# Tanh forms of Gelu and sigmoid tile by tile, state-space units with second buffers, and output low parts on VectorE, in a one-core hybrid layer

## The chip, the cores and the metric

The kernel runs on one core of one Trainium2 chip. The metric is the time of one execution on the device in microseconds, the median of several runs. Engines are named as the profile names them: PE is TensorE (matmuls), PEld its loading of weights, DVE VectorE, ACT ScalarE, POOL GpSimd, SP the engine whose queue starts most DMAs.

## The reference, cut to what matters

One layer of a network of width 1024 over 2048 tokens, in float32. One norm and one input projection feed two mixers, whose outputs are normalised, joined, projected by `w_out` and added to the stream; a SwiGLU feed-forward layer and a last norm follow.

```python
h = rmsnorm(x, norm_mix_g); proj = h @ w_in          # u_ssm 512 | q 512 | k 512 | v 512
# mixer A: 32 groups of 16 channels, one diagonal complex state of 64 per group
_, states = lax.associative_scan(combine, (a, bu), axis=1)
y = einsum(states, c_mat).real + d_skip * uf
y = jax.nn.gelu(y)                                   # the tanh form
y_ssm = y * jax.nn.sigmoid(y @ w_glu + b_glu)
# mixer B: 8 heads of 64, each chunk of 64 tokens sees itself and the 8 chunks before it
y_att = softmax(q k / 8 + bias) v
mixed = concat(rmsnorm(y_ssm, g_ssm), rmsnorm(y_att, g_att))
x = x + mixed @ w_out
h2 = rmsnorm(x, norm_ffn_g)
x = x + (silu(h2 @ w_gate) * (h2 @ w_up)) @ w_down
return rmsnorm(x, norm_final_g)
```

## The kernel before, in words

Nearly every matmul is done in three passes on high and low parts, so that float32 accuracy is kept: `split` makes the high part with a cast on ACT (L165) and the low part as a difference on DVE or POOL (L166), and `mm3` issues high x high, high x low and low x high. All PE matmuls are recorded at L74, transposes and spreads at L77.

The 2048 tokens are four blocks of 512 (`sb`). The program has these stages, with their place in the span in microseconds: the first projections (to about 155), attention with the state-space units and the later projections in between (155 to 743), the mixing (685 to about 950), gate and up (to 1840) and down (to 2303). A tile framework schedules the instructions of each engine by the order of the program and by due times; the matmuls of attention are kept in the order of the program. A pool reuses a tile's space when the last reader of the tile is done, and a transfer into the tile waits for that.

**Attention** (`att_phase`) is a hand-written loop of 128 steps, each one head of a quarter block: scores, masked softmax (`mn` on DVE L846, exponentials on ACT L849), transposes into `pt`, its parts `pth` (ACT L864) and `ptl` (DVE L865), and after four steps the product with v. Between these pieces the loop advances `Unit`s: generators with `n` yields that are spread over the steps `s0` to `s1`, the first piece `pre` steps earlier. Units compute the projections of later blocks, the state-space scan, and, at the end, the first part of the mixing.

**State-space units** (`ssm_unit`, eight of them, b = 0 to 7, four groups each): load U (the inputs), Bst, Tm and Vm; matmuls U x Bst into PSUM `pj`, copied by ACT to X (8 copies, L591); a recursion over 256 chunks of 8 tokens on POOL (L605 to L608 and L616, L617) in 7 + 7 + 3 + 4 pieces; X is moved by POOL's DMA queue into XG; matmuls U x Tm and XG x Vm, copied by ACT to Y (2 copies, L649) and stored to `y`. Before, each of these tiles has one buffer, and Y is a second tile under the tag of X. A unit starts every SW = 15 steps and spans 15. SP issues the loads of a unit when its first piece is run; Tm and Vm are loaded with U.

**Mixing** (`mix_phase`). For each block: `load` fetches y (`yr`) and applies Gelu into `ys`, `split` makes `gh`, `gl`; `load_a` fetches attention's output `ya` and `squares` sums its squares; `glu` multiplies by w_glu (parts `wgh`, `wgl`), adds the bias `bg`, takes the sigmoid and multiplies `ys`; `rstd1` sums squares by matmuls with ones and finds the reciprocal root by Newton steps on DVE (L115 to L123, result `no`); `rstd2` scales by gain; `mixed` makes the parts `m`; `split_wo` makes the parts `woh`, `wol` of w_out once; `w_out` multiplies and adds x. The matmuls of block 0's and 1's GLU write to the banks `pf` and `big`. The tag `sg` is a ring of SGB = 2 temporaries of 128x512, used by w_glu's raw tiles, by the squares and by sigmoid.

In blocks 0 and 1 Gelu is one ACT instruction over 128x2048 (L1034), and the sigmoid is `late`: DVE adds the bias into `yr` (L1061), one ACT instruction over 128x2048 does the sigmoid (L1063), and DVE multiplies (L1065). In blocks 2 and 3 both are done tile by tile (L1034, L1068, L1069). Gelu, sigmoid and the exponential of softmax lie in different tables of ACT, so that a change between them brings an ACT_TABLE_LOAD into ACT's order. The mixing's unit is opened at step OPEN = 119; its loads are issued at once, its pieces from GSTART = 122 on.

Of the kernel before, what the change touches and what calls it, by code (L numbers as in the profile page):

```python
# [12 lines left out]
AF = mybir.ActivationFunctionType  # L13
ALU = mybir.AluOpType
AX = mybir.AxisListType

P = 128
# [3 lines left out]
NG, CH, NS = 32, 16, 64  # L21
NPR = NG // 2
L = 8
NC = SEQ // L
GB, GP = 4, 2
H, HD = 8, 64
SB = 512
# [4 lines left out]
EPS = 1e-6  # L32
LAG = 2
WB = 3
OPEN, GSTART = 119, 122
R1 = 13
SGB = 2
ON_POOL = 2, 5, 7
RA1, RA2 = 2, 12
# [5 lines left out]
SL = 1  # L45
LPH = 2
V0 = 0, 4
DB, XB = 3, 2
SW = 15
CUT = -8, -2, 2, 7, 13, 19, 24  # L50
CUTL = -8, -2, 2, 7, 13, 19, 23
ORDER = "sptf"
# [1 line left out]
YL = 8  # L54
YX = 9
# [51 lines left out]
def f32(ap):  # L107
    return ap.bitcast(F32)
# [54 lines left out]
def split(k, hi, lo, raw, lo_eng=None, hi_eng=None):  # L163
    nc = k.nc
    (hi_eng or nc.scalar).copy(hi, raw)  # L165
    (lo_eng or nc.gpsimd).tensor_tensor(lo, raw, f32(hi), op=ALU.subtract)  # L166
# [393 lines left out]
def ssm_unit(k, p, psum, S, b, eng):  # L560

    nc = k.nc
    F = GB * CH
    U = k.t(p, "U", [P, GB, NC])

    def load(out, in_):
        ins = nc.sync.dma_start(out, in_)
        if b == 0:
            k.tc.keep_in_program_order(ins)
# [7 lines left out]
    for i in range(L):  # L577
        load(tm[i * CH : (i + 1) * CH], S["kt"].rearrange("c g a m -> c g (a m)")[:, gs, P - CH * i : 2 * P - CH * i])
    vm = k.t(p, "Vm", [P, GB, P])
    load(vm[:], S["v"].rearrange("q g c n m -> (c n) (q g) m")[:, gs, CH:])  # L580
# [39 lines left out]
    for s in range(1, 8):  # L620
        step(Xk[:, :, :, :, s], Xk[:, :, :, :, s - 1], 0, NC // 8)
        yield
    for b_ in range(1, 8):
        step(Xe[:, :, :, :, b_], Xe[:, :, :, :, b_ - 1], 1, 4)
        yield
# [13 lines left out]
            eng.dma_start(XGv[c * NS : (c + 1) * NS, :, g2, 1:], X[g2 * NS : (g2 + 1) * NS, c, :, : NC - 1])  # L639
    for _ in range(YX):  # L640
        yield
    Y = k.t(p, "X", [P, GB, NC])
    for q in range(GP):
        ps = k.t(psum, "pj", [P, 2, NC], bufs=2)
        for g2 in range(2):
            g = 2 * q + g2
# [6 lines left out]
        yield  # L653


SSM_N = YL + GP + 7 + 7 + 3 + 4  + YX + GP


class Unit:
# [21 lines left out]
def att_phase(k, ident, S):  # L681
    tc, nc, io = k.tc, k.nc, k.io
    with ExitStack() as cx:
# [245 lines left out]
        sp = tc.alloc_tile_pool(name="ssm", reuse_waits="tile", bufs=1)  # L929
        psum = cx.enter_context(tc.tile_pool(name="aps", bufs=1, space=bass.MemoryType.PSUM, reuse_waits="tile"))  # L930
        psum2 = cx.enter_context(tc.tile_pool(name="aps2", bufs=1, space=bass.MemoryType.PSUM, reuse_waits="tile"))
        units = []
# [9 lines left out]
                      Unit(qk_unit(sb, 2), QK_N, g0 + C[3], g0 + C[4], 2, light=LIGHT), Unit(v_unit(sb, 1), V_N, g0 + C[4], g0 + C[5], 2, light=LIGHT),  # L942
                      Unit(qk_unit(sb, 3), QK_N, g0 + C[5], g0 + C[6], 2, light=LIGHT)]
        for b in range(NG // GB):
            units.append(Unit(ssm_unit(k, sp, psum, S, b, k.ssm_eng), SSM_N, 2 + int(SW * b), 2 + int(SW * (b + 1)), light=SL))
# [24 lines left out]
MIX_N = 17 + PY + PZ  # L970


def mix_phase(k, S, bank):

    tc, nc, io = k.tc, k.nc, k.io
    te = k.te
    with ExitStack() as cx:
# [28 lines left out]
        def squares(src):  # L1006
            sq = k.t(mz, "sq", [P, SB], bufs=2)
            for f in range(4):
                if f == 0:
                    nc.scalar.activation(sq[:], src[f], AF.Square)  # L1010
                else:
                    t = k.t(mz, "sg", [P, SB], bufs=SGB)
                    nc.scalar.activation(t[:], src[f], AF.Square)
                    (nc.gpsimd if f == 2 else nc.vector).tensor_tensor(sq[:], sq[:], t[:], op=ALU.add)
            return sq

# [2 lines left out]

        yrs = [None]  # L1020

        def load(sb, one=False):
# [8 lines left out]
            yv = b.yr = yrs[0][:, :, :, (sb % 2) * 64 : (sb % 2 + 1) * 64]  # L1031
            fs = [slice(0, 4)] if one else [slice(f, f + 1) for f in range(4)]
            for s in fs:
                nc.scalar.activation(yt[:, s].rearrange("p f (c j) -> p f c j", j=L), yv[:, s].rearrange("p f j c -> p f c j"), AF.Gelu_apprx_tanh)  # L1034
# [12 lines left out]
        def glu(b, bank, late=False):  # L1047


            def by8(a):  # L1050
                return a.rearrange("p (a b) -> p a b", a=L)

            for f in range(4):
                ps = bank()
                cs = slice(f * P, (f + 1) * P)
                for q in range(4):
                    mm3(te, ps[:, :512], Wg[q][0][:, cs], Wg[q][1][:, cs], b.g[q][0][:], b.g[q][1][:], q == 0, q == 3)
                    if q < 3:
                        yield
                if late:  # L1060
                    nc.vector.tensor_scalar(b.yr[:, f], by8(ps[:, :512]), bg[:, f : f + 1], None, op0=ALU.add)  # L1061
                    if f == 3:
                        nc.scalar.activation(b.yr, b.yr, AF.Sigmoid)  # L1063
                        for i in range(4):
                            nc.vector.tensor_tensor(by8(b.ys[i]), by8(b.ys[i]), b.yr[:, i], op=ALU.mult)  # L1065
                else:
                    sg = k.t(mz, "sg", [P, SB], bufs=SGB)
                    nc.scalar.activation(sg[:], ps[:, :512], AF.Sigmoid, bias=bg[:, f : f + 1])  # L1068
                    nc.vector.tensor_tensor(b.ys[f], b.ys[f], sg[:], op=ALU.mult)  # L1069
                yield  # L1070
            b.sqs = squares(b.ys)

        def rstd1(b, c, ps):

# [73 lines left out]
        b = load(0, True)  # L1148
# [4 lines left out]
        for n, _ in enumerate(glu(b, bank, True)):  # L1153
# [7 lines left out]
        nxt = load(1, True)  # L1161
        for _ in range(PZ):
            yield

# [2 lines left out]
            psum = k.psum  # L1167
            return bank() if psum is None else big()

        for n, _ in enumerate(glu(nxt, bk, True)):  # L1170
            if n == R1:
                rstd1(b, 1, bk())
            yield
# [531 lines left out]
```

## Time and profile before

| | before |
|---|---|
| time, median of 3 runs | 2308.74 us (2308.12 to 2310.45) |
| the profiled execution's own time | 2304.9 us |
| its span | 2303.1 us |
| mean granted clock of TensorE | 0.975 |
| busy PE / PEld / DVE / ACT / POOL | 2183.8 / 1834.1 / 1487.8 / 1001.3 / 1061.0 us |
| bytes moved by DMA | 437 MB, mean 190 GB/s |

The profile is of one execution. In its lists, a line has the line of the program, engine, operation, output and inputs, shape, and how many; a timeline has start and length in microseconds, and in brackets how long the engine was idle before, and what ended it. A table of waits has engine, waiting line, what it waited for, and then the total in microseconds, the number and the longest. The granted clock is a share of full speed.

### The profile page before, as it was taken

The numbers are of one execution on the slowest core, as the hardware profiler recorded it, in microseconds if no ns is written. First come the engines' busy times: TensorE is split into PE (matmuls) and PEld (weight loads), VectorE is DVE, ScalarE is ACT, GpSimd is POOL, SyncE is SP. The second block draws the span as 40 slices with busy tenths as digits, with TensorE's granted clock in tenths as the row PEclk, the third lists the DMA queues.
The fourth block names the chain that finished last, engine by engine and source line by source line (L and its number), as shares of the span: only waits on it lengthen the run. The fifth ranks groups of instructions, "written<-read, shape, count | busy, mean of one in ns | idle before, by whom it ended". The sixth has DMA issues, their size and how long they took to land.

```text
span 2303.1 us, 30454 instructions
## 1 busy us (share of the span) xinstructions
PE 2183.8 (95%) x10568; PEld 1834.1 (80%) x10568; DVE 1487.8 (65%) x2286; ACT 1001.3 (43%) x1675; POOL 1061.0 (46%) x1245
## 2 busy tenths in 40 slices
PE   8978799999997899989999999999999999999997
PEld 6667688898986788778888887888888878888886
DVE  7845555656555756676775669766645376578676
ACT  6335555555557542343333335333333343344332
POOL 3416655455660433265555554555555314445442
PEclk9989999999998999999999999999999999999998
DMA  8788766766653534754554556555433287465552
GB/s 295 260 286 265 235 210 204 207 190 193 192 137 114 178 118 163 249 165 143 167 193 157 205 190 254 195 193 167 158 96 110 76 326 265 165 228 183 201 182 74
DMA packets 216370, 437.00 MB, mean 190 GB/s; under 512 B 27352, under 2 KB 58120, under 8 KB 209112
## 3 DMA queue, kind: packets, MB, share of 16 engines
q1 hardware_dynamic: 211352, 420.89, 55.0%
q0 software_dynamic: 4864, 14.17, 1.9%
q8 instruction: 83, 1.36, 0.2%
q14 instruction: 71, 0.58, 0.1%
HBM read 294.98 MB, written 132.15 MB: 185 GB/s over the span
## 4 chain that ended last, share of the span: by engine, by line
PE 59%; DVE 3%; DMA 1%; ACT 1%; issue 1%; POOL 1%; SPq 0%; DVEq 0%; ACTq 0%; POOLq 0%
PE X L74 20%; PE ps L74 18%; PE Y L74 10%; PE big L74 6%; PE W L74 5%; DVE acc L1575 1%; DMA lo<-hc 0%; DMA x<-xt 0%; DVE xt L1117 0%; DVE lo L166 0%; DVE hd L166 0%; POOL c L166 0%; ACT hi L165 0%; POOL sa L1125 0%; DMA gl<-x 0%
## 5 line engine op out<-in xcount | busy, mean ns | idle before, releaser
L74 PE MATMUL X<-hi,c 128*128 128x512 f32 x1408 | 452.2, 392 | 7.6 <-ACT u L1391 3.5
L74 PE MATMUL ps<-hd,hd 128*128 128x512 f32 (+1 forms) x1968 | 431.7, 381 | 3.9 <-DVE hd L166 3.7
L74 PEld LDWEIGHTS ps<-hd,hd 128*128 128x128 f32 x1968 | 358.8, 190 | 75.5 <-DVE hd L166 5.1
L166 POOL TENSOR_TENSOR c<-S,c 128x512 fp32r<-128x512 f32 x176 | 253.1, 1440 | 260.7 <-ACT c L165 258.8
L74 PEld LDWEIGHTS X<-hi,c 128*128 128x128 f32 x1408 | 265.8, 189 | 65.2 <-ACT u L1391 5.1
L74 PE MATMUL X<-lo,c 128*128 128x512 f32 x704 | 275.3, 391 | 0.0
L166 POOL TENSOR_TENSOR hd<-hd 128x1536 fp32r<-128x1536 f32 (+1 forms) x46 | 159.1, 3463 | 232.0 <-ACT hd L165 218.8
L166 POOL TENSOR_TENSOR c<-raw,c 128x512 fp32r<-128x512 f32 x132 | 189.0, 1432 | 137.5 <-ACT c L165 109.1
L165 ACT CAST hd<-hd 128x1536 fp32r<-128x1536 f32 (+1 forms) x106 | 147.4, 1393 | 219.4 <-DMA hd<-hq 134.5
L74 PE MATMUL Y<-hi,c 128*128 128x512 f32 x704 | 225.5, 391 | 4.8 <-DVE u L1395 4.8
L1521 DVE TENSOR_TENSOR acc<-acc,ps 128x512 f32<-128x512 f32 x196 | 129.2, 681 | 79.5 <-PE ps L74 79.1
L74 PE MATMUL big<-m,woh 128*128 128x512 f32 x512 | 165.4, 404 | 0.6 <-DVE m L166 0.4
L165 ACT CAST c<-S 128x512 fp32r<-128x512 f32 x176 | 109.5, 622 | 116.5 <-PE Y L74 59.1
L74 PE MATMUL pf<-hi,w 128*128 128x512 f32 x416 | 150.9, 415 | 9.4 <-ACT hi L729 5.8
L74 PEld LDWEIGHTS Y<-hi,c 128*128 128x128 f32 x704 | 132.6, 188 | 33.9 <-DVE u L1395 6.3
L74 PEld LDWEIGHTS X<-lo,c 128*128 128x128 f32 x704 | 133.0, 189 | 27.7
L1391 ACT COPY u<-X 128x512 f32<-128x512 f32 x132 | 77.1, 585 | 177.5 <-PE X L74 177.5
L846 DVE CUSTOM_DVE_ANT_0 s<-sc,nb 128x640 f32<-128x640 f32 (+4 forms) x128 | 94.4, 737 | 89.4 <-PE sc L74 85.9
L605 POOL TENSOR_TENSOR st<-X,a 128x128 f32<-128x128 f32 (+2 forms) x136 | 47.4, 349 | 220.0 <-ACT X L591 157.4
L165 ACT CAST c<-raw 128x512 fp32r<-128x512 f32 x132 | 82.1, 622 | 143.1 <-PE Y L74 80.3
L166 DVE TENSOR_TENSOR hd<-hd 128x1536 fp32r<-128x1536 f32 (+1 forms) x60 | 119.3, 1990 | 31.2 <-ACT hd L165 30.5
L74 PE MATMUL Y<-lo,c 128*128 128x512 f32 x352 | 137.2, 390 | 0.0
(462 smaller groups left out, 4644.2 us busy)
## 6 DMA issues: line engine op xcount, KB each, us to landing
w<-wss SPq DMA_DIRECT2D x36, 1024.0 KB, 5.5
hq<-g SPq DMA_DIRECT2D x140, 256.0 KB, 2.1
hd<-hq SPq DMA_DIRECT2D x42, 768.0 KB, 4.5
hd<-wc SPq DMA_DIRECT2D x42, 768.0 KB, 6.0
raw<-in_w_gate SPq DMA_DIRECT2D x44, 512.0 KB, 3.7
raw<-in_w_up SPq DMA_DIRECT2D x44, 512.0 KB, 4.1
wc<-px SPq DMA_DIRECT2D x66, 256.0 KB, 3.2
wss<-w SPq DMA_DIRECT2D x12, 1024.0 KB, 5.6
```

What stands on the lines that cost most here:

```text
L74: return self.tc.keep_in_program_order(self.tc.nc.tensor.matmul(*a, **b))
L165: (hi_eng or nc.scalar).copy(hi, raw)
L166: (lo_eng or nc.gpsimd).tensor_tensor(lo, raw, f32(hi), op=ALU.subtract)
L605: eng.tensor_tensor(t[:, :, :, :n], src, ar, op=ALU.mult)
L846: nc.vector.tensor_tensor_reduce(s[:, :nk].rearrange("p (a b) -> p a b", a=nch), ps[:, :nch, :half], hd.nb[:, nk - 1 :: -1].rearrange("p ( ...
L1391: nc.scalar.copy(u[:], ps[:])
L1521: V.tensor_tensor(a, a, ps[:], op=ALU.add)
L1575: nc.vector.scalar_tensor_tensor(v, v, k.go[:, i : i + 1], self.rs[:, : self.n], op0=ALU.mult, op1=ALU.mult)
```

## The change

It has five parts, made at once.

1. The state-space units: U gets two buffers, Y a tile of its own; a unit starts every 14 steps and spans 15, so that neighbours overlap by one step; the first piece of units 1 to 7, the loads of U and Bst, is run four steps early; their Tm and Vm are loaded after the first seven pieces of the recursion; seven empty yields fall away.
2. The mixing's unit starts at step 121 instead of 122 with fewer empty yields, and its window ends one step earlier; the units' pool is released at step 119 instead of 122.
3. Gelu is computed per tile of 128x512 as y(1 + tanh(c(y + 0.044715 y^3))), twice its value: Square and Tanh on ACT, two scalar-tensor-tensor instructions on DVE, of which the second writes with a step of eight elements; the factor 0.5 goes into `gh` and `gl`. The sigmoid becomes 1 + tanh(z/2), twice its value, straight from PSUM for all blocks, with one DVE instruction per tile. The gain `gs` is scaled by 0.25 and the bias by 0.5 for this. The late path is removed. Temporaries come from the ring `sg`.
4. The low parts of w_out (four of eight) and of `m` (16 of 32) that POOL computed move to DVE.
5. The scratch space of POOL's DMA queue is set to 8192 bytes.

ACT's order holds nine ACT_TABLE_LOADs before and two after. Every line number of the changed kernel is one or more higher (L74 becomes L75, L1034's place is taken by L1044 to L1047).

```diff
-OPEN, GSTART = 119, 122
-R1 = 13
+OPEN, GSTART = 119, 121
+R1 = 9
+CUBE = 0.044715
-SW = 15
+SW, SPAN = 14, 15
...
-    U = k.t(p, "U", [P, GB, NC])
+    U = k.t(p, "U", [P, GB, NC], bufs=2)
...
-    tm = k.t(p, "Tm", [P, GB, P])
...
-    for _ in range(YL):
+    if b == 0:
+        tm, vm = load_tv()
+    for _ in range(YL if b == 0 else 1):
         yield
...
         step(Xk[:, :, :, :, s], Xk[:, :, :, :, s - 1], 0, NC // 8)
         yield
+    if b:
+        tm, vm = load_tv()
...
-    Y = k.t(p, "X", [P, GB, NC])
+    Y = k.t(p, "Y", [P, GB, NC])
...
-            units.append(Unit(ssm_unit(...), SSM_N, 2 + int(SW * b), 2 + int(SW * (b + 1)), light=SL))
+            s0 = 2 + SW * b
+            units.append(Unit(ssm_unit(...), SSM_N if b else SSM_N + YL - 1, s0, s0 + SPAN, 4 if b else 0, light=SL))
...
-                units += [Unit(islice(mix, MIX_N), MIX_N, GSTART, N + LAG, GSTART - OPEN)]
-            if s == GSTART:
-                sp.release()
+                sp.release()
+                units += [Unit(islice(mix, MIX_N), MIX_N, GSTART, N + 1, GSTART - OPEN)]
...
-PY, PZ = 8, 1
-MIX_N = 17 + PY + PZ
+PY, PZ = 3, 1
+MIX_N = 16 + PY + PZ
...
+        nc.vector.tensor_scalar(gs[:], gs[:], 0.25, None, op0=ALU.mult)
+        nc.vector.tensor_scalar(bg[:], bg[:], 0.5, None, op0=ALU.mult)
...
-                split(k, W[q][0][:], W[q][1][:], raw[:], nc.vector if n % 2 else nc.gpsimd)
+                split(k, W[q][0][:], W[q][1][:], raw[:], nc.vector)
...
-                nc.scalar.activation(yt[:, s].rearrange(...), yv[:, s].rearrange(...), AF.Gelu_apprx_tanh)
             for f in range(4):
+                t = k.t(mz, "sg", [P, L, SB // L], bufs=SGB)
+                nc.scalar.activation(t[:], yv[:, f], AF.Square)
+                nc.vector.scalar_tensor_tensor(t[:], t[:], 1 / CUBE, yv[:, f], op0=ALU.add, op1=ALU.mult)
+                nc.scalar.activation(t[:], t[:], AF.Tanh, scale=CUBE * math.sqrt(2 / math.pi))
+                nc.vector.scalar_tensor_tensor(b.ys[f].rearrange("p (c j) -> p j c", j=L), t[:], 1.0, yv[:, f], op0=ALU.add, op1=ALU.mult)
-                split(k, gh[:], gl[:], b.ys[f], nc.vector)
+                nc.scalar.activation(gh[:], b.ys[f], AF.Copy, scale=0.5)
+                nc.vector.scalar_tensor_tensor(gl[:], b.ys[f], 0.5, f32(gh[:]), op0=ALU.mult, op1=ALU.subtract)
...
-                if late:
-                    nc.vector.tensor_scalar(b.yr[:, f], by8(ps[:, :512]), bg[:, f : f + 1], None, op0=ALU.add)
-                    if f == 3:
-                        nc.scalar.activation(b.yr, b.yr, AF.Sigmoid)
-                        for i in range(4):
-                            nc.vector.tensor_tensor(by8(b.ys[i]), by8(b.ys[i]), b.yr[:, i], op=ALU.mult)
-                else:
-                    nc.scalar.activation(sg[:], ps[:, :512], AF.Sigmoid, bias=bg[:, f : f + 1])
-                    nc.vector.tensor_tensor(b.ys[f], b.ys[f], sg[:], op=ALU.mult)
+                nc.scalar.activation(sg[:], ps[:, :512], AF.Tanh, bias=bg[:, f : f + 1], scale=0.5)
+                nc.vector.scalar_tensor_tensor(b.ys[f], sg[:], 1.0, b.ys[f], op0=ALU.add, op1=ALU.mult)
-            b.sqs = squares(b.ys)
+            b.sqs = squares(b.ys, 0.25)
...
-                split(k, mh, ml, y, nc.gpsimd if n % 2 else nc.vector)
+                split(k, mh, ml, y, nc.vector)
...
-        load_wg()
-        yield
+        load_wg()
...
-    nc = bacc.Bacc("TRN2", target_bir_lowering=False, num_devices=1)
+    nc = bacc.Bacc("TRN2", target_bir_lowering=False, num_devices=1, dynamic_dma_scratch_size=8192)
```

Two places where the order of the instructions changes. The first is ACT at the boundary of two state-space units (X from L591, Y from L649, whose tile is still called X before; pth and s belong to attention, v and k to later projections). Before:

```order
L649 COPY X_4155<-pj_4156 128x512
L649 COPY X_4155<-pj_4162 128x512
L864 CAST pth_4124<-pt_4185 128x5x128
L849 ACTIVATE s_4181,sm_3828<-s_4181,mn_4182 128x640
...
L804 CAST v_1008_4071<-pf_4247 128x4x64
L591 COPY X_4308<-pj_4309 64x256 x4
L591 COPY X_4308<-pj_4316 64x256 x4
L849 ACTIVATE s_4330,sm_4236<-s_4330,mn_4331 128x640
```

After:

```order
L657 COPY Y_4063<-pj_4064 128x512
L857 ACTIVATE s_4039,sm_3876<-s_4039,mn_4040 128x640
L657 COPY Y_4063<-pj_4070 128x512
L597 COPY X_4084<-pj_4085 64x256 x4
L597 COPY X_4084<-pj_4092 64x256 x4
L872 CAST pth_3981<-pt_4114 128x5x128
```

The copies of the outgoing unit and those of the incoming one stood apart, with attention's exponentials between; now they follow each other, and one pth stands behind all ten.

The second is DVE from the end of block 0's GLU on (ptl of attention, gl of block 1, yr the bias added for block 0). Before:

```order
L865 TENSOR_TENSOR ptl_8526<-pt_8600,pth_8525 128x5x128
L1061 TENSOR_SCALAR yr_8351<-pf_8584,bg_8214 128x8x64
L166 TENSOR_TENSOR gl_1991_8634<-ys_8631,gh_1990_8633 128x512
L166 TENSOR_TENSOR gl_1993_8638<-ys_8631,gh_1992_8637 128x512
L166 TENSOR_TENSOR gl_1995_8642<-ys_8631,gh_1994_8641 128x512
```

After, where sq and sg are squares and temporaries of the ring, and ys_8647 is block 1's output of Gelu:

```order
L1024 TENSOR_TENSOR sq_8636<-sq_8636,sg_8644 128x512
L1045 SCALAR_TENSOR_TENSOR sg_8648<-sg_8648,yr_8273 128x512
L1045 SCALAR_TENSOR_TENSOR sg_8657<-sg_8657,yr_8273 128x512
L1047 SCALAR_TENSOR_TENSOR ys_8647<-sg_8648,yr_8273 128x8x64
L1047 SCALAR_TENSOR_TENSOR ys_8647<-sg_8657,yr_8273 128x8x64
L1050 SCALAR_TENSOR_TENSOR gl_1999_8654<-ys_8647,gh_1998_8653 128x512
```

Before, the four gl of block 1 follow at once on block 0's last bias; now block 1's Gelu, four tiles of two instructions each, stands in front of its gl, behind the squares of block 0.

More of the change, by code (lines that the diff above doesn't have):

```diff
@@ L575, in ssm_unit, with load_tv @@
     load(bst[:].rearrange("p g m -> p (g m)"), S["bst"][b // 2][:, (b % 2) * GB * P : (b % 2 + 1) * GB * P])
-    tm = k.t(p, "Tm", [P, GB, P])
[L577 to L580, printed above, removed]
-    for _ in range(YL):
+    def load_tv():
+        tm = k.t(p, "Tm", [P, GB, P])
+        for i in range(L):
+            load(tm[i * CH : (i + 1) * CH], S["kt"].rearrange("c g a m -> c g (a m)")[:, gs, P - CH * i : 2 * P - CH * i])
+        vm = k.t(p, "Vm", [P, GB, P])
+        load(vm[:], S["v"].rearrange("q g c n m -> (c n) (q g) m")[:, gs, CH:])
+        return tm, vm
+    if b == 0:
+        tm, vm = load_tv()
+    for _ in range(YL if b == 0 else 1):
         yield
@@ L653, in ssm_unit @@
         yield
-SSM_N = YL + GP + 7 + 7 + 3 + 4  + YX + GP
+SSM_N = 1 + GP + 7 + 7 + 3 + 4  + YX + GP
 class Unit:
@@ L944, in att_phase @@
         for b in range(NG // GB):
-            units.append(Unit(ssm_unit(k, sp, psum, S, b, k.ssm_eng), SSM_N, 2 + int(SW * b), 2 + int(SW * (b + 1)), light=SL))
+            s0 = 2 + SW * b
+            units.append(Unit(ssm_unit(k, sp, psum, S, b, k.ssm_eng), SSM_N if b else SSM_N + YL - 1, s0, s0 + SPAN, 4 if b else 0, light=SL))
         N = len(steps)
@@ L1003, in split_wo, with squares @@
                 raw = raws[n] if n < len(raws) else load_wo(n, wr, "xt")
-                split(k, W[q][0][:], W[q][1][:], raw[:], nc.vector if n % 2 else nc.gpsimd)
-        def squares(src):
+                split(k, W[q][0][:], W[q][1][:], raw[:], nc.vector)
+        def squares(src, scale=1.0):
             sq = k.t(mz, "sq", [P, SB], bufs=2)
@@ L1009, in squares @@
                 if f == 0:
-                    nc.scalar.activation(sq[:], src[f], AF.Square)
+                    nc.scalar.activation(sq[:], src[f], AF.Square, scale=scale)
                 else:
                     t = k.t(mz, "sg", [P, SB], bufs=SGB)
-                    nc.scalar.activation(t[:], src[f], AF.Square)
+                    nc.scalar.activation(t[:], src[f], AF.Square, scale=scale)
                     (nc.gpsimd if f == 2 else nc.vector).tensor_tensor(sq[:], sq[:], t[:], op=ALU.add)
@@ L1020, in mix_phase, with load @@
         yrs = [None]
-        def load(sb, one=False):
+        def load(sb):
             b = B()
@@ L1030, in load @@
                     nc.sync.dma_start(yrs[0][:, f], S["y"][f * P : (f + 1) * P, :, sb * 64 : sb * 64 + 128])
[L1031 to L1034, printed above, removed]
+            yv = yrs[0][:, :, :, (sb % 2) * 64 : (sb % 2 + 1) * 64]
             for f in range(4):
+                t = k.t(mz, "sg", [P, L, SB // L], bufs=SGB)
[3 more added lines that the diff above has]
+                nc.vector.scalar_tensor_tensor(b.ys[f].rearrange("p (c j) -> p j c", j=L), t[:], 1.0, yv[:, f], op0=ALU.add, op1=ALU.mult)
                 gh, gl = k.t(my, f"gh{f}", [P, SB], F32R), k.t(my, f"gl{f}", [P, SB], F32R)
-                split(k, gh[:], gl[:], b.ys[f], nc.vector)
+                nc.scalar.activation(gh[:], b.ys[f], AF.Copy, scale=0.5)
+                nc.vector.scalar_tensor_tensor(gl[:], b.ys[f], 0.5, f32(gh[:]), op0=ALU.mult, op1=ALU.subtract)
                 b.g.append((gh, gl))
@@ L1045, in load_a, with glu @@
             b.sqa = squares(b.ya)
-        def glu(b, bank, late=False):
-            def by8(a):
-                return a.rearrange("p (a b) -> p a b", a=L)
+        def glu(b, bank):
             for f in range(4):
@@ L1144, in mix_phase @@
         load_wg()
-        yield
         mw = rx.enter_context(tc.tile_pool(name="mw", reuse_waits="tile", bufs=2, side="right"))
         wr = rx.enter_context(tc.tile_pool(name="wr", reuse_waits="tile", bufs=2, side="right"))
-        b = load(0, True)
+        b = load(0)
         load_a(b, 0)
@@ L1152, in mix_phase @@
             yield
-        for n, _ in enumerate(glu(b, bank, True)):
+        for n, _ in enumerate(glu(b, bank)):
             if n == RA1:
@@ L1160, in mix_phase @@
             yield
-        nxt = load(1, True)
+        nxt = load(1)
         for _ in range(PZ):
@@ L1168, in bk @@
             return bank() if psum is None else big()
-        for n, _ in enumerate(glu(nxt, bk, True)):
+        for n, _ in enumerate(glu(nxt, bk)):
             if n == R1:
```

2 lines of the change are left out of this document (1 added, 1 removed).

## The prediction

> **What bounds the kernel now.** I read the page first, then the table of waits of TensorE, then the stages in windows, then the timelines of single engines where TensorE stood still. From the page, engine shares and the 40 slices:
>
> ```profile
> PE 2183.8 (95%) x10568; PEld 1834.1 (80%) x10568; DVE 1487.8 (65%) x2286; ACT 1001.3 (43%) x1675; POOL 1061.0 (46%) x1245
> PE   8978799999997899989999999999999999999997
> ```
>
> TensorE is the bound: 95% busy, and its order is fixed. A gain must come from the few slices below 9, and the change touches only work up to slice 16 (a slice is 57.6 us). What TensorE waits for there, and how the stages stand (columns: us, then busy time of PE, PEld, DVE, ACT, POOL, granted clock, DMA share, GB/s):
>
> ```profile
> PE pt L77 <- DVE ptl L865: 13.5, 10, 2.6
> PE pf L74 <- ACT gh L165: 6.8, 1, 6.8
> PE big L77 <- DVE no L123: 5.1, 1, 5.1
> PE big L74 <- POOL sa L1125: 2.3, 1, 2.3
> ...
> 155.00:640.00 485.00, 452.93 (x2735) 403.34 (x2733) 281.90 (x538) 266.91 (x571) 257.67 (x616) 0.98 0.69 210
> 744.00:768.00 24.00, 18.20 (x82) 14.17 (x81) 22.91 (x33) 14.63 (x19) 16.96 (x7) 0.98 0.56 201
> 768.00:790.00 22.00, 20.74 (x94) 16.72 (x93) 16.64 (x22) 16.98 (x27) 7.79 (x5) 0.95 0.49 151
> 790.00:910.00 120.00, 119.49 (x556) 99.54 (x555) 66.02 (x150) 42.33 (x60) 38.06 (x27) 0.99 0.41 132
> 910.00:950.00 40.00, 37.30 (x159) 30.25 (x159) 36.91 (x69) 8.57 (x12) 15.21 (x10) 0.93 0.65 216
> ```
>
> From 790 to 910 TensorE has no idle time (119.49 of 120.00), so the tanh forms of blocks 2 and 3, whose instructions lie there, cost nothing: TensorE's matmuls hide them. Were that cover gone, each block would show its VectorE rows, some 12 us. Four places remain, and the sum has a term for each: the units beside attention, the end of attention with the first GLU, the second GLU, and 925 to 950.
>
> **Term 1, the state-space units beside attention.** With one buffer of U, Tm and Vm, unit b+1 cannot load before unit b's last matmul. TensorE's timeline (start, length, idle before):
>
> ```profile
> 235.47 1.75 PE L74 MATMUL pj<-U,Bst 128*128 128x256 f32 x7 [1.14 <-DMA Tm<-kts]
> 307.25 1.97 PE L74 MATMUL pj<-U,Bst 128*128 128x256 f32 x8 [1.60 <-DMA U<-u]
> 369.26 1.10 PE L74 MATMUL pj<-U,Bst 128*128 128x256 f32 x4 [0.64 <-DMA Tm<-kts]
> 642.88 2.70 PE L74 MATMUL pj<-U,Bst 128*128 128x256 f32 x8 [2.72 <-DMA U<-u]
> ...
> 640.00:655.00 15.00, 12.28 (x77) 11.42 (x76) 5.02 (x10) 7.19 (x18) 7.32 (x15) 0.89 0.58 167
> ```
>
> U is now double and loaded four steps early, and Tm and Vm come after Bst's matmuls and seven recursion steps: 1.14 + 1.60 + 0.64 + 2.72 = 6.1 us of waits go. The last also costs clock: its eight matmuls took 2.70 us where those at 307.25 took 1.97, and the granted clock is 0.89 over 640 to 655 against 0.98 for the whole stage, 15 x 0.09 = 1.4 us, which go too (bounds 0 and 2.7, twice that, if the other units' waits cost clock as well). The DMA issues stay on SP's queue, eight U, Bst, Tm and Vm groups as before; they only move earlier, past the mask and hidden-state loads, which TensorE does not wait for in the table.
>
> Against that, the last unit now ends at step 115 and not 122. Its eight Tm and Vm matmuls leave a stretch where TensorE idles for one where it is busy: 8 times 0.21 us, 1.7 us (bounds 0 and 3.3). And the order puts the outgoing unit's Y next to the incoming unit's X. In ScalarE's order at a unit boundary, shown with the change, two bursts that stood about three steps apart are one, and pth, for which VectorE's ptl and then TensorE wait, stands behind it. The rows by form:
>
> ```profile
> L591 ACT COPY X<-pj 64x256 f32<-64x256 f32 x64 | 23.5, 367 | 14.7 <-issue 6.1 <-PE pj L74 4.3 <-DMA Tm<-kts 3.6
> L649 ACT COPY X<-pj 128x512 f32<-128x512 f32 x16 | 9.4, 586 | 17.6 <-PE pj L74 15.7 <-issue 1.9
> ```
>
> The burst grows from 8 x 0.37 = 2.9 us to 4.1 us. ScalarE is 55% busy in this stage (266.91 of 485), so most of the extra 1.17 us is taken up by slack; I take 0.2 us at each of seven boundaries, 1.5 us (bounds 0 and 8.2, all of it). Term 1: -6.1 - 1.4 + 1.7 + 1.5 = -4.3 us.
>
> **Term 2, from the last unit to the end of the first GLU (698 to 739.7).** ScalarE's timeline, and TensorE's row that waits for it:
>
> ```profile
> 707.59 1.28 ACT L1034 ACT_TABLE_LOAD   x1
> 708.88 3.64 ACT L1034 ACTIVATE ys<-yr 128x2048 f32<-128x2048 f32 x1
> 712.95 2.16 ACT L165 CAST gh<-ys 128x512 fp32r<-128x512 f32 x4
> 716.07 3.83 ACT L1034 ACTIVATE ys<-yr 128x2048 f32<-128x2048 f32 x1
> ...
> 713.61 0.79 PE L74 MATMUL pf<-gh,wgh 128*128 128x512 f32 x1 [6.76 <-ACT gh L165]
> 739.29 0.40 PE L74 MATMUL pf<-gh,wgl 128*128 128x512 f32 x1
> ...
> 690.00:714.00 24.00, 13.06 (x72) 11.15 (x71) 10.83 (x20) 17.29 (x28) 0.00 (x0) 0.75 0.85 277
> 714.00:744.00 30.00, 27.69 (x136) 23.16 (x136) 20.83 (x46) 20.92 (x28) 1.28 (x1) 0.86 0.02 5
> ```
>
> One Gelu over four tiles, behind a table load, holds TensorE for 6.76 us; that wait goes, because y is complete earlier and the first tile needs only a Square, a tanh and two VectorE rows. Half-rate clock (0.75 and 0.86 in the last two rows) shrinks with it: 0.12 of 30 us are 3.6 us lost behind 714, of which I take about half, 1.7. New is the tile chain: its four tiles are ready over about 10 us, against 4.5 us for the first, and the last three make TensorE wait an estimated 3.9 us inside the first GLU group. Term 2: -6.76 - 1.7 + 3.9 = -4.6 us (bounds -8.5, no wait for the tiles, and 0).
>
> The table loads lie inside this term and are not added to it. The load at 707.59 ends at 708.87 and the Gelu starts at 708.88. [...]
>
> **Term 3, the second GLU and the first w_out (739.7 to 767.4).** Block 1's Gelu is done at 716.07 to 719.9 before, long ahead of its use. Now it uses the ring of two temporaries that the squares of block 0 hold, and it stands behind them on ScalarE and VectorE. In VectorE's order behind the first GLU, shown with the change, the low parts gl that TensorE needs stood right behind the first GLU's last row; now they end a chain. Its prices:
>
> ```profile
> L1034 ACT ACTIVATE ys<-yr 128x512 f32<-128x512 f32 x8 | 8.6, 1123 | 3.2 <-POOL m L166 3.2
> L1013 ACT ACTIVATE sg<-ys 128x512 f32<-128x512 f32 x12 | 7.4, 632 | 5.3 <-DVE ys L1069 4.7 <-DVE sq L1014 0.6
> ...
> 743.61 2.50 DVE L1065 TENSOR_TENSOR ys<-ys,yr 128x512 f32<-128x512 f32 x4
> 771.31 1.40 DVE L1082 SCALAR_TENSOR_TENSOR ys<-ys,gs,big 128x512 f32<-128x512 f32 x2
> 752.85 2.76 DVE L166 TENSOR_TENSOR wol<-xt,woh 128x1024 fp32r<-128x1024 f32 x1
> 754.89 6.34 POOL L166 TENSOR_TENSOR wol<-m,woh 128x1024 fp32r<-128x1024 f32 x2 [0.36 <-ACT woh L165]
> 762.23 2.30 DVE L116 CAST nf<-nv 128x4 f32<-128x4 int32 x1
> 767.07 0.16 DVE L123 SCALAR_TENSOR_TENSOR no<-nf,ny 128x4 f32<-128x4 f32 x1
> 770.18 1.22 DVE L166 TENSOR_TENSOR wol<-xt,woh 128x1024 fp32r<-128x1024 f32 x1
> ```
>
> Count from T, the end of the first GLU. Tanh, product, squares and the sum on POOL take until T+4.2. Then VectorE has 14 rows: 8 of 0.70 us (771.31), 2 sums of 0.63 (743.61) and 4 that write in steps of eight elements. The row nearest to such a write is the Gelu of 128x512, whose input is strided: 1123 ns against 632 for Square, so I take 1.2 us (bounds 0.70 and 1.4, twice). That makes 5.6 + 1.3 + 4.8 = 11.7, with 0.9 for tanh and gh between: T+16.8, the last gl. Behind it, up to the last `no`: 4 m of 0.63, 4 ys of 0.70, 8 wol of 1.17 (770.18, started every 1.13), 3 sums, 14 small rows of 0.17: 2.5 + 2.8 + 9.4 + 1.9 + 2.4 = 19.0. So `no` comes at T+35.8. Before it came at 767.23, T+27.5 with T = 739.69. TensorE has no other work then (its 5.1 us wait for `no`), so term 3 is +8.3 us (bounds +2, if VectorE runs wol rows while it waits for tanh, and +10).
>
> [...]
>
> **Term 4, 925 to 950.** POOL's two m of this block ran beside VectorE, whose rows swell:
>
> ```profile
> 930.88 3.49 DVE L1315 TENSOR_TENSOR yr<-yr 128x512 f32<-128x512 f32 x2
> 934.28 1.78 DVE L1317 TENSOR_TENSOR gl<-gl,yr 128x512 f32<-128x512 f32 x1
> 933.77 3.44 POOL L166 TENSOR_TENSOR m<-ys,m 128x512 fp32r<-128x512 f32 x2
> 937.68 0.68 DVE L166 TENSOR_TENSOR m<-ys,m 128x512 fp32r<-128x512 f32 x1
> ...
> q0 software_dynamic: 4864, 14.17, 1.9%
> ```
>
> Four rows swell from 0.68 to about 1.76 us, 4.3 us; four m more on VectorE cost 2.7. Of the 1.6 us net, and of POOL's earlier sa, for which TensorE waits 2.3 us, I take -2.0 us (bounds -2.3 and +2.7). The smaller scratch for POOL's DMA queue is taken as 0: q0, that queue, moves 14.17 MB in 4864 packets in the whole run, 1.9% of the DMA engines' time; a gain is excluded, since less room removes no work, and as an upper bound I take one more wait as long as the longest of term 1's, 2.7 us.
>
> **Sum.** -4.3 - 4.6 + 8.3 - 2.0 = -2.6 us. The profiled execution took 2304.9 us (span 2303.1), 3.8 below the median of 2308.74. Applied to the median: 2306.1 us, 0.11% below, less than the 0.2% (4.6 us) that a measurement of this kernel can tell from no change. I forecast no change.
>
> **Rivals.**
> - Faster by the second GLU: VectorE runs wol and m rows in the gaps, and term 3 shrinks to its bound of +2. For: VectorE is 22.91 of 24.00 busy there, of which contention with POOL is a large part. Against: the order lists the chain ahead of them. 2306.1 - 6.3 = 2299.8.
> - Faster by attention: the merged burst costs nothing (-1.5), the last unit's matmuls nothing (-1.7), and half of the 13.5 us of ptl waits near the units goes with them, say -2.5 more. Against: most of those waits belong to other units. 2306.1 - 5.7 = 2300.4.
> - Slower: the wol rows of 2.76 us are slow from the weight loads that land beside them (DMA share 0.56), not from POOL, and all eight stay so on VectorE: 8 x 1.55 = +12.4, 2318.5. It decides from 2.1 us a row on (8 x 0.91 = +7.3, 0.2% over 2308.74). For: the CAST at 762.23, tiny, took 2.30. Against: POOL was busy in each such row, and the wol at 770.18 took 1.22 at a DMA share of 0.49.
>
> [...]
>
> **How the numbers follow.** No change 0.34 (the likeliest single case); faster by the second GLU 0.21 and by attention 0.18; slower 0.27, in which the upper bounds of the burst (+6.7) and of term 4 also count. That gives faster 0.39, same 0.34, slower 0.27. The forecast's own range is 2304 to 2313; the 8 in 10 range reaches into both faster cases and, at the other end, to most of the slower one: 2294 to 2316.
>
> **What would show it.** Right: no U or Tm waits in the table; no wait for gh at the first GLU; a new wait of big for gl of 6 to 10 us behind the first GLU, `no` at T+34 to T+37; strided ys rows near 1.2 us; wol rows at 1.22. Wrong: pt waits at unit boundaries grown by over 3 us in sum, wol rows over 2 us, or VectorE waiting for ScalarE in the gelu chain so that it takes over 17 us.

## The result, and the profile after

The change made the kernel slower: 2347.47 us against 2310.45 (medians of five runs side by side), a ratio of 1.0165 (95% interval 1.0151 to 1.0179). The forecast was 2306.1 in a range of 2294 to 2316. The profiled execution has a span of 2345.7 us, 42.6 more than before. From the page after, shares and slices:

```profile
PE 2198.3 (94%) x10568; PEld 1843.6 (79%) x10568; DVE 1511.7 (64%) x2332; ACT 996.8 (42%) x1696; POOL 1023.7 (44%) x1225
PE   8978689898997799989999999999999999999997
```

TensorE does the same 10568 matmuls and is busy 2198.3 us where it was 2183.8, but some of the slices from the fifth on, attention, are emptier. The stage of attention after (columns: us, busy time of PE, PEld, DVE, ACT, POOL, granted clock, DMA share, GB/s), and what TensorE waits for in the whole run (total, number, longest):

```profile
155.00:640.00 485.00, 427.18 (x2488) 376.35 (x2487) 258.17 (x495) 243.01 (x526) 255.41 (x616) 0.94 0.64 196
```

```profile
PE sc L75 <- DVE k L783: 11.8, 3, 7.3
PE pf L75 <- DMA w<-wss: 10.5, 5, 3.5
PE pf L75 <- ACT hi L737: 10.2, 5, 3.8
PE pf L75 <- ACT gh L1049: 9.6, 1, 9.6
PE big L78 <- DVE no L124: 4.5, 1, 4.5
PE pj L75 <- DMA XG<-X: 3.7, 1, 3.7
```

The waits for U and Tm are gone, as forecast. In their place stand waits of the projections (`pf`) for weights (w) and for x (hi), and waits of the scores (`sc`) for k: `w<-wss` was not in the table before, the wait for hi was 5.8 us and that for k 6.8. In 155 to 640 TensorE was busy 427 us where it had been 453, at a clock of 0.94 instead of 0.98.

Where the time went is best read step by step. For the n-th exponential of softmax (ACT L849 before, L857 after), counted from 0, the table gives its start before, and how much later it starts in after and in the experiments below, each from the profile of one execution:

| exponential no. | 12 | 16 | 32 | 60 | 96 | 120 |
|---|---|---|---|---|---|---|
| before, start in us | 204.1 | 217.3 | 295.9 | 421.8 | 584.4 | 689.9 |
| after, later by | 1.1 | 9.6 | 23.3 | 34.6 | 41.8 | 42.8 |
| e1: all but units and steps | -0.2 | -0.2 | 0.4 | -0.5 | -0.6 | -0.5 |
| e2: units alone | 1.8 | 10.9 | 27.7 | 34.7 | 41.2 | 42.3 |
| e4: units, 15 steps | -0.8 | 10.2 | 13.5 | 13.1 | 19.5 | 16.3 |
| e5: second buffers alone | 1.9 | 6.0 | 5.6 | 9.6 | 17.0 | 11.9 |
| e3: after, Y stored by POOL | 1.9 | 11.2 | 20.9 | 27.0 | 22.1 | 21.5 |
| e6: after, loads not early | 0.2 | 0.4 | 22.5 | 22.7 | 25.7 | 26.5 |
| e7: after, Tm with U | 0.7 | 10.5 | 20.9 | 36.3 | 47.1 | 48.0 |
| e13: after, unit transfers by POOL | 1.6 | 1.7 | 3.9 | 6.0 | 1.6 | 1.1 |
| e14: units alone, transfers by POOL | 0.7 | 0.9 | 8.4 | 9.9 | 5.6 | 5.0 |

All 42.8 us are lost beside attention, most of it in jumps near the boundaries of units; from there to the end nothing net. Differences of a few us in the table mean little: where the units are those of before, no. 120 stands at -0.5 (e1), but also at +3.0 (e9), +4.5 (e10) and +3.4 (e15). No. 60 lies on a boundary: e13 is 6.0 late there and 0.8 at no. 66.

The first boundary, on SP's queue (start, length, issue), before:

```profile
210.64 1.87 SPq L693 DMA_DIRECT2D raw<-in_w_qk  x2
215.62 0.93 SPq L714 DMA_DIRECT2D xt<-in_xt  x2
224.10 0.33 SPq L567 DMA_DIRECT2D U<-u  x1
225.15 3.61 SPq L652 DMA_DIRECT2D y<-X  x8
228.80 4.08 SPq L567 DMA_DIRECT2D U<-u  x7
```

and after:

```profile
211.59 2.79 SPq L568 DMA_DIRECT2D U<-u  x4
215.40 0.95 SPq L710 DMA_DIRECT2D wss<-w  x2
230.34 3.60 SPq L660 DMA_DIRECT2D y<-Y  x8
233.98 0.90 SPq L701 DMA_DIRECT2D raw<-in_w_qk  x2
```

U can be loaded early now, and with it the order of SP's queue changes: the stores of unit 0's Y stand ahead of the raw weights of the next projection, and SP sits from 216.35 to 230.34 waiting for Y. The weights are issued at 233.98 instead of 210.64. On TensorE, one row before and three after:

```profile
221.24 0.67 PE L74 MATMUL pj<-XG,Vm 128*128 128x256 f32 x2 [1.45 <-DMA XG<-X]
...
224.74 0.67 PE L75 MATMUL pj<-XG,Vm 128*128 128x256 f32 x2 [3.69 <-DMA XG<-X]
242.02 0.50 PE L75 MATMUL pf<-hi,w 128*128 128x512 f32 x1 [2.45 <-ACT w L166]
270.29 0.80 PE L75 MATMUL pf<-hi,w 128*128 128x512 f32 x1 [3.81 <-ACT hi L737]
```

Three things come one after the other. The first 8 us, at no. 16 and 17, stand before the late weights are needed: TensorE waits 3.69 us for XG where it waited 1.45, although POOL issued the moves at nearly the same time (the last from 217.50, before from 217.13), and the matmuls of unit 1 with Bst now come ahead of the scores behind exponential 17. Which transfers made XG land later was not separated. The late weights then cost 3.0 us at 242.02 (2.45 and 0.53), while the lag stays at 8 us, since the kernel before has its wait for Tm there. The next jump, from 9.4 us at no. 25 to 17.7 at no. 26, lies at waits for hi and lo, which are made from x: 9.6 us in four waits from 265 to 281, at a granted clock of 0.65 (262 to 290). In e13, with the units' transfers off SP's queue, the lag at no. 26 is -0.4 us.

### The profile page after: what moved, and what is told of

The parts are those of the page before. It is cut to its first block, busy times and chain, and to the rows that moved or that the text cites. A ratio compares the mean times of both kernels' runs of the same rounds, so it can differ in the third digit from the quotient of the medians.

```text
span 2345.7 us, 30460 instructions
## 1 busy us (share of the span) xinstructions
PE 2198.3 (94%) x10568; PEld 1843.6 (79%) x10568; DVE 1511.7 (64%) x2332; ACT 996.8 (42%) x1696; POOL 1023.7 (44%) x1225
## 4 chain that ended last, share of the span: by engine, by line
PE 73%; DVE 9%; issue 6%; DMA 6%; POOL 3%; ACT 3%; SPq 1%; DVEq 0%; POOLq 0%; ACTq 0%
PE X L75 19%; PE ps L75 18%; PE Y L75 9%; PE pf L75 7%; PE big L75 7%; PE W L75 5%; PE pj L75 4%; PE sc L75 2%; PE pt L78 2%; DMA xt<-in_xt 2%; DMA w<-wss 1%; DVE lo L167 1%; DVE acc L1576 1%; ACT X L597 0%; DVE cm L89 0%
## 5 line engine op out<-in xcount | busy, mean ns | idle before, releaser
L75 PE MATMUL X<-hi,c 128*128 128x512 f32 x1408 | 451.8, 392 | 6.8 <-DMA hq<-g 3.4
L75 PE MATMUL ps<-hd,hd 128*128 128x512 f32 (+1 forms) x1968 | 431.8, 381 | 3.8 <-DVE hd L167 3.7
L75 PEld LDWEIGHTS ps<-hd,hd 128*128 128x128 f32 x1968 | 358.8, 190 | 75.4 <-DVE hd L167 5.3
L75 PEld LDWEIGHTS X<-hi,c 128*128 128x128 f32 x1408 | 265.9, 189 | 64.3 <-ACT u L1392 4.9
L75 PE MATMUL X<-lo,c 128*128 128x512 f32 x704 | 275.1, 391 | 0.0
L75 PE MATMUL Y<-hi,c 128*128 128x512 f32 x704 | 226.1, 392 | 5.2 <-DVE u L1396 5.2
L75 PE MATMUL pf<-hi,w 128*128 128x512 f32 x416 | 154.7, 424 | 16.9 <-ACT hi L737 10.2
L75 PE MATMUL big<-m,woh 128*128 128x512 f32 x512 | 163.2, 401 | 0.0
L75 PEld LDWEIGHTS Y<-hi,c 128*128 128x128 f32 x704 | 133.0, 189 | 34.5 <-DVE u L1396 6.8
L75 PEld LDWEIGHTS X<-lo,c 128*128 128x128 f32 x704 | 132.8, 189 | 27.4
L75 PE MATMUL Y<-lo,c 128*128 128x512 f32 x352 | 137.7, 391 | 0.0
```

Of the source, the lines that this page charges most:

```text
L75: return self.tc.keep_in_program_order(self.tc.nc.tensor.matmul(*a, **b))
```

## The experiments

Each is a short edit; a ratio is to the kernel before, timed on the same chip (its median there 2309 to 2312). The edits are shown by the lines that matter, those of e1 and e2 in short form. The smaller scratch space of POOL's queue is in all of them but e9 and was not tried alone; e12 and e14 have it and stand within 0.1% of before.

**Which part loses.** e1 is after with the units and the mixing's steps of before; e2 is before with the units alone.

```diff
e1 -SW, SPAN = 14, 15; U bufs=2; tag "Y"; early loads; OPEN, GSTART = 119, 121; PY = 3
e1 +SW = 15; ...; OPEN, GSTART = 119, 122; PY = 8
e2 (before) +SW, SPAN = 14, 15; U bufs=2; tag "Y"; U and Bst 4 steps early; Tm and Vm after the recursion
```

> The changed kernel with its state-space units and the start of the mixing as before: only the tanh forms, the low parts on DVE and the scratch size. The changed kernel reached attention step 120 some 43 us later than the kernel before and ended 42.6 us later, so all of the loss came up beside the units. Theory A (SP's queue is held by stores and loads of the units) and B (14 steps are too close for a unit): both expect this kernel within 5 us of before, 2305 to 2315. Rival C (the tanh forms or the low parts slow attention too): over 2325.

> The kernel before with only the units changed (second U, own Y, 14 steps apart, U and Bst four steps early, Tm and Vm after the first recursion) and the scratch size. A and B: the whole loss, 2340 to 2355. C: below 2320.

Measured: e1 2320.96, 1.0055 (1.0040 to 1.0070); e2 2343.86, 1.0158 (1.0142 to 1.0175). The units cost 34.6 us. e1 leaves attention untouched (its row of the table), so C falls for attention; but it is 11.7 us slower than before, above the 2315 that was expected; in its profile (of its fastest execution, 2314.77) what is lost stands behind attention.

**What in the units.** e3 moves the stores of Y to POOL's queue; e4 is e2 with 15 steps; e6 is after without the early start; e7 is after with Tm and Vm loaded early; e8 is e4 with e3's edit.

```diff
e3 -nc.sync.dma_start(S["y"][...], Y[...])
e3 +nc.gpsimd.dma_start(S["y"][...], Y[...])
e4 -SW, SPAN = 14, 15
e4 +SW, SPAN = 15, 15
e6 -Unit(ssm_unit(...), ..., s0, s0 + SPAN, 4 if b else 0, light=SL)
e6 +Unit(ssm_unit(...), ..., s0, s0 + SPAN, 0, light=SL)
e7 -    if b == 0:
e7 -        tm, vm = load_tv()
e7 +    tm, vm = load_tv()
e7 ...
e7 -    if b:
e7 -        tm, vm = load_tv()
```

> The changed kernel with the stores of Y to y on POOL's queue instead of SP's. In the changed kernel SP waited 29.5 us for ACT's Y at these stores (L660, 8 waits, longest 13.9 us), with the weight and x loads of the projections behind it. Theory A1 (these stores are what holds SP): 2347 falls by 20 us or more, to 2310 to 2327, and the waits of pf for w and hi shrink. A2 (the many early loads of U, Tm and Vm hold SP) and B: less than 8 us better, 2340 or more.

> As the kernel before with only the units changed, but 15 steps apart (SW = 15, SPAN = 15, so no overlap of neighbours). Theory B (14 steps and the overlap are the cause): back to 2305 to 2315. A1 and A2 (queue order): hardly better than with 14 steps, 2335 to 2350.

> The changed kernel (2347) with the first piece of units 1 to 7, the loads of U and Bst, at the unit's start instead of four steps early. A2 (these nine loads stand among the x and weight loads of the projections on SP): 2325 to 2340, and the waits of pf for w and hi shrink. A1 (the stores of Y) and B (the spacing) alone: 2343 to 2351.

> The changed kernel with Tm and Vm loaded with U and Bst, as before the change, instead of after seven pieces of the recursion. If the late place of Tm and Vm is part of the loss (nine issues that fall among the projections' loads): 2335 or less. If not, 2342 to 2351; if early loads of Tm wait on SP for the outgoing unit's matmuls, over 2352.

> The kernel before with the units' change, 15 steps apart, and the stores of Y on POOL's queue. 15 steps took 17 us off the 35 and the stores on POOL's queue took 16 off the changed kernel. If they are two causes: the loss goes, 2306 to 2315. If they are one cause (with 15 steps the stores come when Y is there): 2322 to 2328.

Measured: e3 2331.30, 1.0097 (1.0083 to 1.0111); e4 2326.39, 1.0075 (1.0059 to 1.0092); e6 2334.35, 1.0098 (1.0083 to 1.0114); e7 2352.06, 1.0179 (1.0162 to 1.0196); e8 2319.65, 1.0034 (1.0022 to 1.0045). Each of three edits takes 13 to 18 us off, and none takes all: none of A1, A2 and B alone is right. e7 is no gain: the late place of Tm and Vm is not part of the loss. e8 lies between the two cases I had set, so the causes overlap. e6's first jump is not gone, it comes one exponential later (11.4 us at no. 17), and it shows the order of the queue most plainly (two rows of SP's queue and one of TensorE):

```profile
223.85 3.58 SPq L660 DMA_DIRECT2D y<-Y  x8
227.48 0.42 SPq L568 DMA_DIRECT2D Bst<-bsts  x1
231.45 3.74 PE L75 MATMUL pj<-U,Bst 128*128 128x256 f32 x8 [8.25 <-DMA Bst<-bsts]
```

The load of Bst stands behind the stores of Y, and TensorE stands still for 8.25 us until it has landed.

**The second buffers alone.** e5 is before with U's second buffer and Y's own tile and nothing else of the units; e11 stores Y by POOL as well; e12 also loads units 1 to 7 by POOL.

```diff
e5  +U = k.t(p, "U", [P, GB, NC], bufs=2)
e5  +Y = k.t(p, "Y", [P, GB, NC])
e11 +nc.gpsimd.dma_start(S["y"][...], Y[...])
e12 +ins = (nc.gpsimd if b else nc.sync).dma_start(out, in_)
```

> The kernel before with nothing but the second buffer of U and Y's own tile (and the scratch size); starts, spans and the place of all loads as before. With all other parts of the units' change the loss beside attention was 35 us (14 steps) and 17 us (15 steps). Prediction's term 1: the waits for U of 4.3 us go, 2303 to 2307. Theory A (the place of loads and stores in SP's queue is what costs): within 4 us of before, 2305 to 2313. Rival: the second buffers themselves pull the stores of Y ahead of the projections' loads, 2315 or more.

> The kernel before with the second buffer of U, Y's own tile and the stores of Y on POOL's queue. The second buffers alone cost 9.5 us; SP's queue then held 13.2 us at the first store of Y with the next loads behind it. Theory A1 (that wait is the cost of the second buffers): back to 2305 to 2313. Rival (U's loads beside the move of X to XG and the projections' loads cost, whoever stores Y): 2316 to 2322.

> As the kernel before with the second buffer and Y's own tile, with the stores of Y and also the loads of units 1 to 7 (U, Bst, Tm, Vm) on POOL's queue, so that SP's queue holds nothing of these units. If SP's queue is the whole cost and the waits for U are a true gain: 2300 to 2307. If POOL's recursion is held by 26 issues a unit (0.62 us each, 16 us): 2315 or more.

Measured: e5 2319.61, 1.0041 (1.0025 to 1.0056); e11 2313.62, 1.0019 (1.0007 to 1.0032); e12 2311.26, 1.0007 (0.9997 to 1.0017). My gain of term 1 did not come: with all else equal U's second buffer and Y's own tile, which e5 has together, cost 0.41%, 9.5 us (8.0 between the medians). SP's waits in e5 from 195 to 330, and SP's queue there:

```profile
SPq L652 <- ACT Y L649: 17.3, 2, 13.2
```

```profile
215.11 2.69 SPq L567 DMA_DIRECT2D U<-u  x5
231.06 3.58 SPq L652 DMA_DIRECT2D y<-Y  x8
234.69 1.90 SPq L567 DMA_DIRECT2D U<-u  x2
242.84 0.44 SPq L714 DMA_DIRECT2D xt<-in_xt  x1
```

The raw weights go out in time here (212.36), but x, which went out at 215.62, now goes at 242.84, behind the stores. Stores by POOL give back about half, between the two cases I had set for e11; with all transfers by POOL no loss clear of noise is left, but no gain either (2300 to 2307 was expected of one).

**Is SP's queue the whole cost?** e13 is after, e14 is e2, each with e12's edit.

> The changed kernel with the stores of Y and the loads of units 1 to 7 (U, Bst, Tm, Vm) on POOL's queue instead of SP's; all else as changed. If SP's queue is the whole cost of the units: 2347 falls by 30 us or more, to 2305 to 2317, and attention's step 120 comes within 6 us of before. If the 14 steps and the merged copies on ACT cost by themselves: 2322 or more.

> The kernel before with the units' change, 14 steps apart, and those transfers on POOL's queue. On SP's queue this cost 34.6 us. If SP's queue is the whole cost: within 5 us of before, 2305 to 2315. If the spacing costs by itself: 2320 or more. The prediction's -4.3 us for the waits for U and Tm that are gone would be 2303 to 2307.

Measured: e13 2307.84, 0.9995 (0.9979 to 1.0011); e14 2306.85, 0.9990 (0.9979 to 1.0002). The loss is gone with nothing changed but the queue that issues 26 small transfers of each unit (of unit 0 only the stores); with them there, the spacing of 14 steps costs nothing. SP issued as many of them before the change, so it is not their number. From 155 to 640 the waits of `pf` for hi, lo and w, w<-wss included, sum to 9.4 us before and to 31.0 after; in e13 they are 4.3, with the wait for XG grown to 5.4 from 1.4:

```profile
PE pj L75 <- DMA XG<-X: 5.4, 3, 3.2
PE pf L75 <- ACT w L166: 3.6, 1, 3.6
PE pf L75 <- DVE lo L728: 0.7, 2, 0.4
```

That it is the order of SP's queue, and not only the place of these transfers, is read from the rows; no run kept all of them on SP with the stores behind the projections' loads. SP's own waits from 195 to 640 show the slack, before, after and in e13:

```profile
SPq L697 <- PE pf L74: 91.2, 24, 7.5
```

```profile
SPq L705 <- PE pf L75: 48.4, 9, 8.7
SPq L660 <- ACT Y L657: 19.4, 6, 13.9
```

```profile
SPq L705 <- PE pf L75: 146.0, 29, 11.2
```

These are waits for TensorE to free a weight buffer, that is, time by which SP is ahead: 91 us before, 48 after, 146 in e13.

**The tanh forms and the low parts.** e9 is before with the low parts alone, e10 before with the tanh forms alone; e15 is e1, and e16 is e13, with a ring of two of Gelu's own.

```diff
e9  -split(..., nc.vector if n % 2 else nc.gpsimd)   # w_out and m
e9  +split(..., nc.vector)
e15 -t = k.t(mz, "sg", [P, L, SB // L], bufs=SGB)
e15 +t = k.t(mz, "tg", [P, L, SB // L], bufs=2)
```

> The kernel before with only the low parts of w_out and of m moved from POOL to DVE. Term 4 of the prediction and the wol rows of term 3: without POOL beside them the rows shrink (2.76 to 1.22), 2 to 5 us faster, 2303 to 2308. Rival: DVE is the longer queue behind the second GLU and its four more wol rows end later, 2312 or more.

> The kernel before with only the tanh forms of Gelu and sigmoid (and the scratch size); low parts on POOL and the mixing's steps as before. Tanh forms and low parts together cost 11.7 us (0.55%). Prediction's term 3: the second Gelu behind the squares costs about 8 us, so 2315 to 2322. Rival (the tanh forms are neutral and the lows cost): 2306 to 2313.

> Tanh forms and low parts with the units and steps of before (2321, +11.7 us), but Gelu's temporaries in a ring of two of its own, so that block 1's Gelu stands during the first GLU on ACT and DVE and not behind block 0's squares. If the shared ring is the cost (term 3 of the prediction): 7 us or more better, 2306 to 2314. If the added DVE instructions are: 2317 or more.

> The changed kernel with both: transfers of units 1 to 7 on POOL's queue and a ring of its own for Gelu. If both are whole causes and the earlier end of the units helps the mixing by the 5.6 us that the changed kernel shows before the first GLU's end: 2295 to 2306, faster than before. If the gains do not add: 2307 to 2315.

Measured: e9 2311.20, 1.0007 (0.9996 to 1.0018), the same; e10 2320.48, 1.0048 (1.0032 to 1.0065); e15 2314.69, 1.0020 (1.0008 to 1.0032), 6.3 us better than e1 by the medians, a little less than the 7 I had asked; e16 2306.94, 0.9991 (0.9979 to 1.0003). So the tanh forms cost beside the old units, the low parts don't, and a ring of its own takes off about half of the 11.7 us of e1. It does not add to e13, which has no such ring and stands at 2307.84.

The profiles show why only half. From the end of the first GLU to `no` e1 takes 36.8 us and e15 27.4, as much as before (27.7): there the shared ring was the whole loss. But e15's first GLU ends 55.5 us after exponential 120, where it was 49.8 before and 50.3 in e1. Block 1's Gelu now stands among attention's last steps; one of its tiles waits on ScalarE for y to be loaded, with an exponential and a pth behind it, and TensorE waits for the ptl made after that:

```profile
738.91 0.63 ACT L1037 ACTIVATE tg<-yr 128x512 f32<-128x512 f32 x1 [2.81 <-DMA yr<-y]
741.84 0.76 PE L78 MATMUL pt<-ident,s 128*128 128x128 f32 x5 [2.95 <-DVE ptl L866]
```

What the other 2 us are was not settled. No version tried is clear of noise below the kernel before; e14 and e16 are the nearest, at -0.10% and -0.09%.

## Why the prediction was wrong

**Term 1 failed, and one sentence of it.** "The DMA issues stay on SP's queue, eight U, Bst, Tm and Vm groups as before; they only move earlier, past the mask and hidden-state loads, which TensorE does not wait for in the table." The issues did not only move earlier. The wait for U had held the stores of Y (225.15 us) and the loads of U (from 224.10) behind the projections' loads; without it they stand ahead of them, and the store that waited 13.9 us for its data held the loads behind it: the raw weights went out at 233.98 us instead of 210.64. And TensorE did wait for them before. The table names only the last to release TensorE, and a load of x reaches it through VectorE and ScalarE, so the wait stands there as one for hi; the rows before:

```profile
260.50 1.45 DVE L728 SCALAR_TENSOR_TENSOR xt<-xt,g_mix,rsn 128x512 f32<-128x512 f32 x2 [1.63 <-DMA xt<-in_xt]
261.95 0.79 PE L74 MATMUL pf<-hi,w 128*128 128x512 f32 x1 [3.45 <-ACT hi L729]
```

These loads had no slack at that place. The term was -4.3 us; it came out at +42.8 (exponential no. 120). The order of SP's queue with what each row waits for would have shown it; the prediction reads ScalarE's and VectorE's orders there and not SP's. Of its three signs of being wrong none points at SP's queue, and the first did not come: the waits of pt for ptl fell from 13.5 to 7.1 us.

The priced parts of term 1 were small beside it. With SP's queue out of the way, e13 stands at +1.1 us at no. 120 and e14, in the slowest of its executions, at +5.0: the waits for U and Tm are gone, but no gain of 4.3 us shows. By the times it is not excluded for e14 (0.9979 to 1.0002, that is -4.8 to +0.5 us), but it is for e12, where the second buffers alone are on POOL's queue (0.9997 to 1.0017). In e13's timeline, new waits stand at the boundaries:

```profile
287.50 0.86 PE L75 MATMUL pj<-XG,Vm 128*128 128x256 f32 x2 [3.23 <-DMA XG<-X]
420.24 1.13 PE L75 MATMUL pj<-U,Bst 128*128 128x256 f32 x4 [1.71 <-ACT Y L657]
```

In sum the waits for XG grew by 4.0 us in e13 and those for the copy to Y, which holds the bank `pj`, by 1.7, about as much as the 6.1 us of waits for U and Tm that went.

**Terms 2 to 4 came near their numbers, but only term 3 by its mechanism.** From after's rows, and the last one from e1:

```profile
776.46 0.40 PE L75 MATMUL pf<-gh,wgl 128*128 128x512 f32 x1
784.48 0.50 PE L75 MATMUL big<-gh,wgh 128*128 128x512 f32 x1 [0.84 <-ACT gh L1049]
790.42 0.79 PE L75 MATMUL big<-gl,wgh 128*128 128x512 f32 x1 [1.21 <-DVE gl L1050]
813.50 1.09 PE L78 MATMUL big<-ident,no 128*128 128x128 f32 x4 [4.49 <-DVE no L124]
...
L1047 DVE SCALAR_TENSOR_TENSOR ys<-sg,yr 128x512 f32<-128x512 f32 x16 | 17.2, 1142 | 0.1
L1045 DVE SCALAR_TENSOR_TENSOR sg<-sg,yr 128x512 f32<-128x512 f32 x16 | 11.0, 692 | 0.2
L167 DVE TENSOR_TENSOR wol<-xt,woh x4: 1218/1221/1226, 794.7 to 811.4; 128x1024 fp32r<-128x1024 f32 x4
...
720.38 1.87 PE L75 MATMUL pf<-ones,sq 128*128 128x1 f32 x8 [6.60 <-DVE sq L1017]
```

- Term 2: the first GLU ends at 776.86 instead of 739.69, 37.2 later, where attention was 42.8 late: -5.6 us (forecast -4.6). That the number is near is luck. The wait for gh did not go; it grew from 6.8 to 9.6 us. In e1, with before's steps, it did go, but TensorE then waits 6.60 us for the sum of squares sq, a wait of 1.5 us before: sq is used at 720.38 where it was 721.26 before, and the first GLU ends where it did before, at 739.7. The removed wait had hidden the next one. The gain comes with the mixing's earlier place: from exponential 120 to the end of the first GLU it is 49.8 us before and 50.3 in e1, but 44.2 in after, 42.7 in e13 and 44.6 in e16. No run has that place alone.
- Term 3: from there to `no` 36.6 us against 27.7, +8.9 (forecast +8.3), and the same in e1 (36.8) and e13 (36.7); e15 takes it away. The last gl is done 14.7 us after the GLU's end (16.8 was priced), and from there to `no` it is 21.8 us (19.0 was priced). The strided write took 1.14 us (1.2 was taken) against 0.69 for its contiguous neighbour. The wait of 6 to 10 us for gl that I had named did not stand as one row; it is split over matmuls from 784 to 791 and the 4.49 us for `no`.
- Term 4: from `no` to the end 1532.2 us against 1535.7, -3.5 (forecast -2.0). No other run repeats it: e1 takes 1536.5 us there, e13 1535.9 and e9, the low parts alone, 1535.7. The gain of this term is not shown.

Of the rivals, the slower one was the wrong mechanism: all eight wol rows took 1.22 us in after, and in e9, where only the low parts moved off POOL, 1.22 too, so it was POOL beside it that had made one take 2.76, not the loads: before, POOL was busy 7.64 of the 8.00 us from 752 to 760, at a DMA share of 1.02; in after it was idle for the 13.00 us from 794 to 807, in which six of the eight rows begin, at a DMA share of 1.05. "Faster by attention" had the right place and the wrong sign.

## What to carry to other kernels

A wait that a change removes also held something back: list what stands behind it in its queue and what will pass, and read the order of that queue itself, with its waits, before pricing the gain. A table of waits names the last to release an engine, so a load can decide and not be named. On SP's queue here a store of Y that waited 13.9 us for its data held the loads behind it, and the raw weights went out at 233.98 us instead of 210.64; keep stores of late results on a queue with nothing urgent behind them. Slack of a queue is visible: the time it waits for its consumers to free a buffer (91 us before, 48 after, 146 in e13).

## What the runs showed that I had not expected

A second buffer of U and a tile of Y's own, 4 KB a partition each, cost 0.41% (0.25 to 0.56), by the order of one queue. Moving some 26 small transfers per unit from SP's to POOL's queue cost nothing that shows in the time, though POOL takes 0.62 us to issue one of its own and runs the recursion: e12 is at 1.0007 (0.9997 to 1.0017). The hazard has moved rather than gone. In e13 POOL's queue stops for 10.22 us before it can load Tm:

```profile
292.34 1.03 POOL L568 DMA_DIRECT2D Tm<-kts  x2 [10.22 <-PE pj L75]
```

What stood behind it there, the stores of Y and the next recursion, could wait.
